# Four steps of weight preparation behind the evictions of a Strassen-Winograd block product, and three operands loaded into their low parts

## The chip, the cores and the metric

The kernel runs on one core of a Trainium2 chip. The metric is the device time of one execution in microseconds; the time before is the median of three runs, 1374.28 us (1374.14 to 1376.15).

## The reference

A two-layer backbone for 1024 latent tokens and 256 context tokens of 1024 channels, in float32: modulated RMS norms, an even layer (a convolution branch and a recurrent branch between one input and one output projection) and an odd layer (pooling). The change touches the even layer's output projection and most of the odd layer's last one:

```python
return jnp.concatenate([y_a, y_b], axis=-1) @ p["w_out"], hT        # even layer
...
z = h @ p["w_in"]                                                   # odd layer
u, g = jnp.split(z, [W_POOL], axis=-1)
...
y = jnp.einsum("bngi,gij->bngj", d, p["w_grp"]).reshape(bn, n, W_POOL) * p["scale"]
return (y * jax.nn.silu(g)) @ p["w_out"]
...
x = x + gate[:, None] * out_x
```

The odd layer's `w_out` is 2048 x 1024. The result must be that of float32 products.

## The kernel before

Activations lie transposed, channels on the 128 partitions and tokens along the row. A float32 product is made of three matmuls on TensorE (PE) in a rounded format, fp32r: each operand v is split into a high part (a cast on ScalarE, ACT, line 95) and a low part v - high (a subtraction on VectorE, DVE, line 96), and high x high, high x low, low x high are summed in PSUM (lines 666, 668, 669).

The large projections are computed in blocks of 256 output channels by 1024 tokens, each by a 2 x 2 Strassen-Winograd scheme: `quad` runs seven products (`prod`, twelve matmuls of 128x512 each) into three PSUM tiles, `qa`, `qb`, `qc` (a, b, c in the code). In the order of the program the products take the weight operands p1, p5, p6, p2, p7, p3, p4 and the token operands b11, t1, t2, b21, t3, b22, t4. Behind most products a PSUM tile is read by `put`, here called an eviction: behind t3's product comes `put(1, 1, b, 1)`, and t4's product, which goes on summing in the same `qb`, must wait for it. Evictions have a high priority. `wquad` prepares the seven weight operands of a block: it loads two raw tiles `wr` of 128x1024, makes sums on DVE (names `ws`, `wr`) and splits seven 128x512 operands (names `wq`). `quad` calls `ahead()`, the preparation of the next block, behind the copy that reads `qa` after the first product (`evac`).

Blocks in order of time: `woa` (layer 1's output projection, first half, m = 0, 2, 4, 6, about 745 to 890 us); then for each of eight m a block `v` and a block `g` of the odd layer's input projection; the weights of these are prepared by `wquad` ahead of the block, not through `ahead`, except that the last `g` block prepares the first block of what follows. The odd layer's output projection has two parts, 1024 input channels each: `wo0` with part 0 (four blocks, m = 0 to 6, from about 1186 us), then `wo1` with part 1 (two blocks in `quad`, the rest in `last_half0` and the code of the end). The evictions are L1088 in `to_gate`, L1150 and L1135 (`gated`) in `wo0`, L1135 in `wo1`.

The token operands of `wo0` and `wo1` come from memory: `y_store` writes the gated blocks and their sums (`y_b`, `y_t`), `y_operand` loads each operand as two raw tiles `yr` of 128x1024 (512 KB) and splits them into `y_<operand>h` and `y_<operand>l`. The raw tiles are taken from a pool shared with other tiles (`xtile`), so a load waits until one is free. All these DMAs are issued by SyncE (SP), in order: an issue that waits holds back all behind it.

A scheduler orders each engine's instructions from the program and from priorities; `tc.issue_after(ins)` keeps what is issued inside it behind `ins` where they are on the same engine. Engines keep that order strictly.

Of the kernel before, what the change touches and what calls it, by code (L numbers as in the profile page):

```python
# [55 lines left out]
def body(ctx, tc, xT, ctxT, cc, ccol, modT, modW, win, gw, wout, wu, grp, wg, wo1, small, edge, ident, outT):  # L56
# [571 lines left out]
    def wquad(src, name, ring, late=False):  # L628
# [17 lines left out]
        nc.vector.tensor_tensor(out=s3, in0=a11, in1=a21, op=sub)  # L646
        nc.vector.tensor_tensor(out=a21, in0=a21, in1=a22, op=add)
# [3 lines left out]
        p6 = op(a11, 6)  # L651
        p2 = op(a12, 2)
        p7 = op(s3, 7)
        nc.vector.tensor_tensor(out=a12, in0=a12, in1=a11, op=sub)
# [5 lines left out]
        return p1, p2, p3, p4, p5, p6, p7  # L660

# [15 lines left out]
    def quad(w, name, ops, put, ahead=None):  # L677
# [14 lines left out]
        w = None  # L692
        if ahead is not None:
            with tc.issue_after(evac.ins):
                w = ahead()
        prod(b, p7, ops["t3"], False, False)
        with tc.high_priority(offset=EVAC):
            put(1, 1, b, 1)
        prod(c, p3, ops["b22"], False, True)
        with tc.high_priority(offset=EVAC):  # L700
            put(0, 1, c, 1)
        prod(b, p4, ops["t4"], False, True)
        with tc.high_priority(offset=EVAC):
            put(1, 0, b, None)
        return w
# [157 lines left out]
    def wo_weights(m):  # L863
        return wquad([wout[m + i, 0] for i in range(2)], f"woa{m}", ring_w)

    w0 = wo_weights(0)
# [16 lines left out]
    def woa(m, w, ahead):  # L883
# [3 lines left out]
        def put(i, h, x, part):  # L887
            v, dr = x1[m + i][:, HALF[h]], x1_part[m + i][:, HALF[h]]
            if part != 1:
                nc.sync.dma_start(v, dr)  # L890
            nc.vector.scalar_tensor_tensor(out=v, in0=x, scalar=m0[:, 0, 2 * KT + m + i : 2 * KT + m + i + 1],
                                           in1=v, op0=mult, op1=add)
            if part != 0:
                nc.sync.dma_start(dr, v)
                square_acc(nacc[h][:, :H], v, (m, i) == (0, h), f"n1q{m}_{i}_{h}")
        return quad(w, f"woa{m}", ya, put, ahead)
# [131 lines left out]

    def y_operand(ops, part, name, raw_tile, alloc):
        hi, lo = [], []  # L1030
        for q in range(2):
            r = raw_tile(f"yr_{part}_{name}_{q}")
            nc.sync.dma_start(r, y_raw[part][name][:, q * S : (q + 1) * S])
            hi.append(alloc(f"y{part}_{name}h{q}", F32R))
            lo.append(alloc(f"y{part}_{name}l{q}", F32R))
            split(r, hi[q], lo[q], nc.vector)
# [5 lines left out]
    def y_operands(part, raws, names=BOPS, alloc=None):  # L1042
        for name in names:
            y_operand(yops[part], part, name, next(raws),
# [12 lines left out]
    def wo1_weights(part, m):  # L1057
        return wquad([wo1[m + i, part] for i in range(2)], f"wo{part}_{m}", wo1_ring,
# [3 lines left out]
    vps, silu = [], [None]  # L1062
    for m in range(0, NK, 2):
# [18 lines left out]
        def to_gate(i, h, x, part):  # L1082
            v = ys[m + i][:, HALF[h]]
            if part == 0:
                keep_part(parts, f"g{m}", i, x)
                return
            if part == 1:
                nc.vector.tensor_tensor(out=v, in0=x, in1=parts[i], op=add)  # L1088
                x = v
            silu[0] = nc.scalar.activation(v, x, AF.Silu)  # L1090

# [16 lines left out]
        if m == NK - 2:  # L1108
            y_operands(0, iter([dtile] + [xtile] * (4 - 1)), BOPS[:4])
# [4 lines left out]
        if m == NK - 2:  # L1114
            with tc.issue_after(silu[0].ins):
                y_operands(0, iter([xtile] * 7), BOPS[4:])
# [21 lines left out]
    for m in range(0, KT, 2):  # L1138
        parts = {}

        def put(i, h, x, part):
# [25 lines left out]
        w = quad(w, f"wo0_{m}", yops[0], put, nxt)  # L1167
        if m == 2:
# [9 lines left out]
    for m in range(0, KT - 4, 2):  # L1178
        def put(i, h, x, part):
            v = x1[m + i][:, HALF[h]]  # L1180
            gated(m + i, v, x)
            if part != 0:
                square_fin(m + i, h, slice(0, H), v)
        def ahead():
# [74 lines left out]
    def last_half0(m, w, ahead=None):  # L1259
# [10 lines left out]
        if ahead is not None:  # L1270
            with tc.issue_after(evac.ins):
                nxt = ahead()
# [159 lines left out]
```

## Time and profile before

| | |
|---|---|
| median of three runs | 1374.28 us (1374.14 to 1376.15) |
| the profiled execution | 1381.07 us, span 1379.3 us, mean granted PE clock 0.974 |
| PE busy | 1295.9 us of the span, 5664 matmuls |
| DVE busy | 1205.1 us, 1587 instructions |
| ACT busy | 632.7 us |
| mean DMA traffic | 132 GB/s |

PE is the engine to watch, but a busy share is a mean over stages: a row of PE whose start is later than the one before it allows, with a wait in brackets behind it, tells where time goes. `<-DVE y L1088` in such a row names the instruction that released it, and why that one was late is read on its own engine. PEclk is the clock that was granted to PE, in tenths or as a share of 1.

### The profile page before, as it was taken

What the parts mean: (1) busy time and instruction counts of PE and PEld (TensorE: products, weight loads), DVE (VectorE), ACT (ScalarE), POOL (GpSimd) and SP (SyncE); (2) the same over time, 40 slices, a digit from 0 to 9 for tenths busy, and PEclk for the clock granted to TensorE, in tenths of its full rate; (3) what the DMA queues carried; (4) which work ended last, traced back from release to release, by engine and by line L of the source; (5) the groups of instructions that cost most, each with busy time, mean ns of one, the idle gap of its engine ahead of it and who ended that gap; (6) DMA issues with size and microseconds to landing.
All of it is one profiled execution on the core that took longest, in us unless ns stands there. A gap on an engine that the chain in (4) does not pass through costs nothing.

```text
span 1379.3 us, 15637 instructions
## 1 busy us (share of the span) xinstructions
PE 1295.9 (94%) x5664; PEld 1048.2 (76%) x5664; DVE 1205.1 (87%) x1587; ACT 632.7 (46%) x906; POOL 363.3 (26%) x182
## 2 busy tenths in 40 slices
PE   7889989898999799999998999999999999999896
PEld 4468868787777587787887887788888888778685
DVE  7998999999999999998778865999999987876775
ACT  6353644674465542304533544754334344634442
POOL 5173534743473555523320004000000000000002
PEclk9899999999999899999999999999999999999997
DMA  9753011111112113343353646424243334758623
GB/s 354 280 180 119 25 59 54 53 40 61 54 35 72 46 46 130 110 151 135 103 185 122 221 154 205 138 93 151 100 145 123 115 115 132 265 190 275 206 107 123
DMA packets 82866, 181.79 MB, mean 132 GB/s; under 512 B 7778, under 2 KB 27618, under 8 KB 82788
## 3 DMA queue, kind: packets, MB, share of 16 engines
q1 hardware_dynamic: 74340, 176.60, 37.8%
q10 hardware_dynamic: 8448, 4.20, 1.0%
q8 instruction: 44, 0.72, 0.2%
q14 instruction: 34, 0.28, 0.1%
HBM read 136.72 MB, written 44.04 MB: 131 GB/s over the span
## 4 chain that ended last, share of the span: by engine, by line
PE 36%; DVE 10%; DMA 7%; issue 2%; ACT 2%; POOL 1%; POOLq 0%; SPq 0%; DVEq 0%; ACTq 0%
PE ga L127 2%; PE ga L128 2%; PE ga L126 2%; PE wob L127 2%; PE wob L128 2%; PE wob L126 2%; DMA wr_g<-wg 1%; DVE ws L986 1%; DMA yr_t<-y_t 1%; DMA wr_v<-wfold 1%; PE qb_g L666 1%; DVE wq_g L96 1%; PE qb_g L669 1%; PE qb_g L668 1%; DVE wq_wo L96 1%
## 5 line engine op out<-in xcount | busy, mean ns | idle before, releaser
L746 DVE SCALAR_TENSOR_TENSOR conv<-u,sm,conv 128x1013 f32<-128x1013 f32 (+14 forms) x232 | 291.2, 1272 | 6.6 <-ACT conv L738 3.8
L1252 POOL TENSOR_TENSOR o<-x,rr 128x256 f32<-128x256 f32 (+1 forms) x9 | 8.0, 923 | 462.9 <-ACT rr L1240 460.0
L511 ACT ACTIVATE g<-g,sm 128x512 f32<-128x512 f32 (+1 forms) x96 | 58.8, 617 | 110.5 <-PE g L510 108.3
L96 POOL TENSOR_TENSOR wl_wu<-wr_wu,wh_wu 128x1024 fp32r<-128x1024 f32 x16 | 39.4, 2470 | 153.9 <-ACT wh_wu L95 147.7
L463 POOL TENSOR_TENSOR g<-g,uc 128x1280 f32<-128x1280 f32 x16 | 47.5, 2967 | 107.9 <-ACT g L511 65.1
L249 PE MATMUL fold<-gh,wh_wu 128*128 128x512 f32 x128 | 53.0, 416 | 5.7 <-ACT wh_wu L95 5.7
L250 PE MATMUL fold<-gl,wh_wu 128*128 128x512 f32 x128 | 52.4, 409 | 3.2 <-DVE gl L96 3.2
L128 PE MATMUL gb<-h0h,wl_gb 128*128 128x512 f32 x128 | 50.7, 398 | 4.8 <-POOL wl_gb L96 4.8
L126 PE MATMUL vg<-h0h,wh_vg 128*128 128x512 f32 x128 | 52.3, 408 | 2.7 <-ACT g L511 2.1
L251 PE MATMUL fold<-gh,wl_wu 128*128 128x512 f32 x128 | 50.7, 405 | 2.3 <-POOL wl_wu L96 2.3
L128 PE MATMUL xb<-h0h,wl_xb 128*128 128x512 f32 x128 | 50.2, 392 | 2.0 <-POOL wl_xb L96 2.0
L127 PE MATMUL wob<-ybl,wh_wob 128*128 128x512 f32 x128 | 50.5, 395 | 1.2 <-POOL ybl L96 1.2
L465 POOL TENSOR_TENSOR g<-g,th 128x1280 f32<-128x1280 f32 x16 | 46.9, 2948 | 16.8 <-ACT th L449 16.8
L127 PE MATMUL vg<-h0l,wh_vg 128*128 128x512 f32 x128 | 51.2, 400 | 0.0
L126 PE MATMUL gb<-h0h,wh_gb 128*128 128x512 f32 x128 | 50.6, 395 | 0.1
L126 PE MATMUL va<-h0h,wh_va 128*128 128x512 f32 x128 | 50.6, 395 | 0.0
L127 PE MATMUL va<-h0l,wh_va 128*128 128x512 f32 x128 | 50.6, 395 | 0.0
L508 PE MATMUL g<-uh,wh_gw 128*128 128x512 f32 (+1 forms) x96 | 36.3, 379 | 15.1 <-ACT wh_gw L95 6.4
L126 PE MATMUL wob<-ybh,wh_wob 128*128 128x512 f32 x128 | 50.6, 396 | 0.0
L128 PE MATMUL wob<-ybh,wl_wob 128*128 128x512 f32 x128 | 49.9, 391 | 0.7 <-POOL wl_wob L96 0.7
L128 PE MATMUL va<-h0h,wl_va 128*128 128x512 f32 x128 | 50.4, 395 | 0.0
L127 PE MATMUL gb<-h0l,wh_gb 128*128 128x512 f32 x128 | 50.4, 393 | 0.0
(548 smaller groups left out, 4301.1 us busy)
## 6 DMA issues: line engine op xcount, KB each, us to landing
mod<-modT SPq DMA_DIRECT2D x28, 512.0 KB, 5.5
wr_wu<-wu SPq DMA_DIRECT2D x16, 512.0 KB, 3.9
x_part<-xp SPq DMA_DIRECT2D x32, 256.0 KB, 2.4
mod<-modT SPq DMA_DIRECT2D x32, 256.0 KB, 3.3
wr_v<-wfold SPq DMA_DIRECT2D x16, 512.0 KB, 3.7
wr_g<-wg SPq DMA_DIRECT2D x16, 512.0 KB, 5.4
wr_wo<-wo SPq DMA_DIRECT2D x16, 512.0 KB, 4.2
yr_t<-y_t SPq DMA_DIRECT2D x16, 512.0 KB, 6.3
```

The lines of the kernel that those rows point to most:

```text
L96: eng.tensor_tensor(out=lo, in0=src, in1=hi.bitcast(F32), op=sub))
L126: nc.tensor.matmul(ps, hi[:, kc], xh[k][:, cols], start=(k == 0), stop=False)
L127: nc.tensor.matmul(ps, hi[:, kc], xl[k][:, cols], start=False, stop=False)
L128: nc.tensor.matmul(ps, lo[:, kc], xh[k][:, cols], start=False, stop=(k == ks - 1))
L249: nc.tensor.matmul(ps, wh[:, kc], gh[i], start=(i == 0), stop=False)
L250: nc.tensor.matmul(ps, wh[:, kc], gl[i], start=False, stop=False)
L251: nc.tensor.matmul(ps, wl[:, kc], gh[i], start=False, stop=(i == 3))
L463: nc.gpsimd.tensor_tensor(out=ius[d], in0=ius[d], in1=uc, op=mult)
L465: nc.gpsimd.tensor_tensor(out=ius[d], in0=ius[d], in1=roots[d], op=mult)
L508: nc.tensor.matmul(ps[:, :n], gwh[:, kc], uh[:, a : a + n], start=True, stop=False)
L511: nc.scalar.activation(t[:, a : a + n], ps[:, :n], AF.Sigmoid, bias=col(ob + d * KT + j))
L746: nc.vector.scalar_tensor_tensor(out=(us[j] if k == 30 else acp)[:, a:b], in0=us[j][:, a + o : b + o], scalar=col(O_CONVW + 31 * j + k), i ...
```

## The change

`wquad` becomes the generator `wquad_steps` with three `yield`s, which cut the preparation into four steps: (1) the loads, p1 and the sum `ws`; (2) two sums, p5 and p6; (3) p2 and p7; (4) one sum, p3 and p4. `quad` runs step 1 behind the copy `evac`, as before, and the later steps behind the evictions of t3's, b22's and t4's products: step 2 behind `put(1, 1, b, 1)`, step 3 behind `put(0, 1, c, 1)`, step 4 behind `put(1, 0, b, None)`. Code that calls `wquad` itself, and `last_half0`, runs all steps in one. In `y_operand` a raw tile can be `None`: the raw operand is then loaded into the tile of its low part and split in place; this is used for t3, b22 and t4 of both parts. Of part 0's operands, t2 and b21 are now issued behind the last gate block (behind its eviction `summed`) and not ahead of it; b21 of part 1 is issued behind the last `wo0` block and not inside its `nxt`; the wait of `nxt` for the last store of y falls away. For this every `put` returns the instruction that reads PSUM, in `woa` too, which the diff leaves out.

```diff
-    def wquad(src, name, ring, late=False):
+    def wquad_steps(src, name, ring, late=False):
         raw = []
...
         nc.vector.tensor_tensor(out=s3, in0=a11, in1=a21, op=sub)
+        yield
         nc.vector.tensor_tensor(out=a21, in0=a21, in1=a22, op=add)
         nc.vector.tensor_tensor(out=a11, in0=a21, in1=a11, op=sub)
         if not late:
             p5 = op(a21, 5)
         p6 = op(a11, 6)
+        yield
         p2 = op(a12, 2)
         p7 = op(s3, 7)
+        yield
         nc.vector.tensor_tensor(out=a12, in0=a12, in1=a11, op=sub)
...
+    class Steps:
+        def __init__(self, work):
+            self.work, self.value = work, None
+        def step(self, after=None):
+            with ExitStack() as octx:
+                if after is not None:
+                    octx.enter_context(tc.issue_after(after.ins))
+                try:
+                    next(self.work)
+                except StopIteration as end:
+                    self.work, self.value = iter(()), end.value or self.value
+        def all(self):
+            while self.value is None:
+                self.step()
+            return self.value
+    def wquad(*args):
+        return Steps(wquad_steps(*args)).all()
...
             put(0, 0, a, None)
-        w = None
-        if ahead is not None:
-            with tc.issue_after(evac.ins):
-                w = ahead()
+        nxt = Steps(ahead()) if ahead is not None else Steps(iter(()))
+        nxt.step(evac)
         prod(b, p7, ops["t3"], False, False)
         with tc.high_priority(offset=EVAC):
-            put(1, 1, b, 1)
+            out = put(1, 1, b, 1)
+        nxt.step(out)
         prod(c, p3, ops["b22"], False, True)
         with tc.high_priority(offset=EVAC):
-            put(0, 1, c, 1)
+            out = put(0, 1, c, 1)
+        nxt.step(out)
         prod(b, p4, ops["t4"], False, True)
         with tc.high_priority(offset=EVAC):
-            put(1, 0, b, None)
-        return w
+            out = put(1, 0, b, None)
+        nxt.step(out)
+        return nxt.all() if ahead is not None else None
...
     def wo_weights(m):
-        return wquad([wout[m + i, 0] for i in range(2)], f"woa{m}", ring_w)
-
-    w0 = wo_weights(0)
+        return wquad_steps([wout[m + i, 0] for i in range(2)], f"woa{m}", ring_w)
+    w0 = Steps(wo_weights(0)).all()
     for name in BOPS[4:]:
...
         for q in range(2):
-            r = raw_tile(f"yr_{part}_{name}_{q}")
-            nc.sync.dma_start(r, y_raw[part][name][:, q * S : (q + 1) * S])
             hi.append(alloc(f"y{part}_{name}h{q}", F32R))
             lo.append(alloc(f"y{part}_{name}l{q}", F32R))
+            r = lo[q].bitcast(F32) if raw_tile is None else raw_tile(f"yr_{part}_{name}_{q}")
+            nc.sync.dma_start(r, y_raw[part][name][:, q * S : (q + 1) * S])
             split(r, hi[q], lo[q], nc.vector)
...
         for name in names:
-            y_operand(yops[part], part, name, next(raws),
+            y_operand(yops[part], part, name, next(raws, None),
                       alloc or (dtile if name in ("b11", "b21", "t4") else d2tile))
...
     def wo1_weights(part, m):
-        return wquad([wo1[m + i, part] for i in range(2)], f"wo{part}_{m}", wo1_ring,
+        return wquad_steps([wo1[m + i, part] for i in range(2)], f"wo{part}_{m}", wo1_ring,
                      part == 1 and m >= KT - 4)
     wo1_ring = wo_ring(iter(["x", "x", "x", "wh", "wl", "wh", "wl"] + ["wh", "wl", "d", "d"] * 14))
-    vps, silu = [], [None]
+    vps, silu, summed = [], [None], [None]
     for m in range(0, NK, 2):
...
                 return
+            out = None
             if part == 1:
-                nc.vector.tensor_tensor(out=v, in0=x, in1=parts[i], op=add)
+                out = summed[0] = nc.vector.tensor_tensor(out=v, in0=x, in1=parts[i], op=add)
                 x = v
             silu[0] = nc.scalar.activation(v, x, AF.Silu)
+            return out
...
         if m == NK - 2:
-            y_operands(0, iter([dtile] + [xtile] * (4 - 1)), BOPS[:4])
+            y_operands(0, iter([dtile, xtile]), BOPS[:2])
         for i in range(2):
             for h in range(2):
                 pool(m + i, h, vps[2 * i + h])
         w = quad(wq, f"g{m}", bx, to_gate, (lambda: wo1_weights(0, 0)) if m == NK - 2 else None)
         if m == NK - 2:
+            with tc.issue_after(summed[0].ins):
+                y_operands(0, iter([xtile] * 2), BOPS[2:4])
             with tc.issue_after(silu[0].ins):
-                y_operands(0, iter([xtile] * 7), BOPS[4:])
+                y_operands(0, iter(()), BOPS[4:])
         for i in range(2):
...
                 x = s
-            gated(m + i, t, x)
+            out = gated(m + i, t, x)
             nc.sync.dma_start(x1_part[m + i][:, HALF[h]], t)
             if (m, i, h) == (0, 0, 1):
                 y_sums(NK - 2)
+            return out
         def nxt():
             if m < KT - 2:
-                with tc.issue_after(stored[0].ins):
-                    return wo1_weights(0, m + 2)
-            w = wo1_weights(1, 0)
-            y_operands(1, iter([xtile]), BOPS[3:4])
-            return w
+                return wo1_weights(0, m + 2)
+            return wo1_weights(1, 0)
         if m == KT - 2:
             with tc.issue_after(loaded[0].ins):
                 y_operands(1, iter([xtile] * 2), BOPS[1:3])
         w = quad(w, f"wo0_{m}", yops[0], put, nxt)
+        if m == KT - 2:
+            y_operands(1, iter([xtile]), BOPS[3:4])
         if m == 2:
...
             v = x1[m + i][:, HALF[h]]
-            gated(m + i, v, x)
+            out = gated(m + i, v, x)
             if part != 0:
                 square_fin(m + i, h, slice(0, H), v)
+            return out
         def ahead():
             if m == 0:
-                y_operands(1, iter([xtile] * 3), BOPS[4:])
-            w = wo1_weights(1, m + 2)
+                y_operands(1, iter(()), BOPS[4:])
+            w = yield from wo1_weights(1, m + 2)
             x2_load(m + 2)
...
             with tc.issue_after(evac.ins):
-                nxt = ahead()
+                nxt = Steps(ahead()).all()
         with tc.issue_after(mm.ins):
```

What the change does to the order, at three places. In the changed file line 1117 is the former L1088, 1152 the former L1120 (the product of gate and pooled tokens), 1167 L1135, 1182 L1150, 1063 L1033 (loads of operands), 1041 L1014 (stores of y), and 648, 649 the former 647, 648.

DVE around the last gate block; `qb_g` and `qc_g` are its PSUM tiles, `y_t2l` and `y_b21l` low parts of part 0's operands, `wq_wo`, `ws_wo` and `wr_wo` the weights of the first `wo0` block. Before:

```order
L96 TENSOR_TENSOR y_t2l_8878<-yr_t_0_8875,y_t2h_8877 128x1024
L647 TENSOR_TENSOR wr_wo_0_1_8974<-wr_wo_0_1_8974 128x512
L96 TENSOR_TENSOR y_t2l_8884<-yr_t_1_8881,y_t2h_8883 128x1024
L96 TENSOR_TENSOR wq_wo_0_1_8976<-wr_wo_0_0_8972,wq_wo_0_1_8976 128x512
L96 TENSOR_TENSOR y_b21l_8890<-yr_b_0_8887,y_b21h_8889 128x1024
L96 TENSOR_TENSOR wq_wo_0_5_8983<-wr_wo_0_1_8974,wq_wo_0_5_8983 128x512
L648 TENSOR_TENSOR wr_wo_0_0_8972<-wr_wo_0_1_8974,wr_wo_0_0_8972 128x512
L96 TENSOR_TENSOR y_b21l_8896<-yr_b_1_8893,y_b21h_8895 128x1024
L1088 TENSOR_TENSOR y_8849<-qc_g_8916,s_g_8957 128x512
L1120 SCALAR_TENSOR_TENSOR y_8849<-vp_6540,sm,y_8849 128x512
L1088 TENSOR_TENSOR y_8850<-qb_g_8917,s_g_8943 128x512
L96 TENSOR_TENSOR wq_wo_0_6_8986<-wr_wo_0_0_8972,wq_wo_0_6_8986 128x512
```

Now:

```order
L96 TENSOR_TENSOR y_t1l_8870<-yr_t_1_8871,y_t1h_8869 128x1024
L646 TENSOR_TENSOR ws_wo_0_8955<-wr_wo_0_0_8948,wr_wo_0_1_8950 128x512
L1152 SCALAR_TENSOR_TENSOR y_8849<-vp_6540,sm,y_8849 128x512
L1117 TENSOR_TENSOR y_8850<-qb_g_8893,s_g_8919 128x512
L648 TENSOR_TENSOR wr_wo_0_1_8950<-wr_wo_0_1_8950 128x512
L1117 TENSOR_TENSOR y_8849<-qc_g_8892,s_g_8933 128x512
L96 TENSOR_TENSOR wq_wo_0_2_8993<-wr_wo_0_0_8948,wq_wo_0_2_8993 128x512
L649 TENSOR_TENSOR wr_wo_0_0_8948<-wr_wo_0_1_8950,wr_wo_0_0_8948 128x512
L1152 SCALAR_TENSOR_TENSOR y_8850<-vp_6549,sm,y_8850 128x512
L96 TENSOR_TENSOR wq_wo_0_5_8973<-wr_wo_0_1_8950,wq_wo_0_5_8973 128x512
```

The two evictions stand ahead of the splits of t2 and b21, which come eight and more rows later, and of the weight splits of steps 2 to 4.

SP at the same time; `y_b_1`, as a target, is a store of y, `yr_t_…_95` and `yr_b_…_96` load t2 and b21, `97`, `98` and `99` are t3, b22 and t4, and `wr_wo_2` is the raw weight of block 2. Before:

```order
L1033 DMA yr_t_0_8875<-y_t_0_95 128x1024
L1033 DMA yr_t_1_8881<-y_t_0_95 128x1024
L1033 DMA yr_b_0_8887<-y_b_0_96 128x1024
L1033 DMA yr_b_1_8893<-y_b_0_96 128x1024
L1033 DMA yr_t_0_9043<-y_t_0_97 128x1024
L1033 DMA yr_t_1_9049<-y_t_0_97 128x1024
L1033 DMA yr_b_0_9055<-y_b_0_98 128x1024
L1033 DMA yr_b_1_9061<-y_b_0_98 128x1024
L1014 DMA y_b_1_100<-y_8849 128x512
L1033 DMA yr_t_0_9067<-y_t_0_99 128x1024
L1014 DMA y_b_1_105<-y_8850 128x512
L1033 DMA yr_t_1_9073<-y_t_0_99 128x1024
```

Now:

```order
L1041 DMA y_b_1_100<-y_8849 128x512
L1063 DMA yr_t_0_9021<-y_t_0_95 128x1024
L1063 DMA yr_t_1_9027<-y_t_0_95 128x1024
L1063 DMA yr_b_0_9033<-y_b_0_96 128x1024
L1063 DMA yr_b_1_9039<-y_b_0_96 128x1024
L1041 DMA y_b_1_105<-y_8850 128x512
L632 DMA wr_wo_2_0_9140<-wo 128x1024
L1041 DMA y_b_1_103<-y_8850 128x512
L1063 DMA y_t3l_9044<-y_t_0_97 128x1024
L632 DMA wr_wo_2_1_9142<-wo 128x1024
L1063 DMA y_t4l_9064<-y_t_0_99 128x1024
L1063 DMA y_t3l_9049<-y_t_0_97 128x1024
```

A store of y stands ahead of t2 and b21, and another two stores and block 2's weights ahead of t3 and t4; b22 comes last, behind the rows shown.

DVE between blocks 2 and 4 of `wo0`; `s_wo_2` is the eviction behind block 2's t3 product, `wq_wo_4` the operands of block 4. Before:

```order
L96 TENSOR_TENSOR wq_wo_4_1_9299<-wr_wo_4_0_9295,wq_wo_4_1_9299 128x512
L96 TENSOR_TENSOR wq_wo_4_2_9312<-wr_wo_4_0_9295,wq_wo_4_2_9312 128x512
L646 TENSOR_TENSOR ws_wo_4_9302<-wr_wo_4_0_9295,wr_wo_4_1_9297 128x512
L1150 TENSOR_TENSOR qc_wo_2_9236<-qc_wo_2_9236,s_wo_2_9277 128x512
L647 TENSOR_TENSOR wr_wo_4_1_9297<-wr_wo_4_1_9297 128x512
L96 TENSOR_TENSOR wq_wo_4_7_9315<-ws_wo_4_9302,wq_wo_4_7_9315 128x512
L648 TENSOR_TENSOR wr_wo_4_0_9295<-wr_wo_4_1_9297,wr_wo_4_0_9295 128x512
L96 TENSOR_TENSOR y_b11l_9378<-yr_b_0_9375,y_b11h_9377 128x1024
L96 TENSOR_TENSOR wq_wo_4_5_9306<-wr_wo_4_1_9297,wq_wo_4_5_9306 128x512
L654 TENSOR_TENSOR wr_wo_4_0_9295<-wr_wo_4_0_9295 128x512
L1150 TENSOR_TENSOR s_wo_2_9263<-qb_wo_2_9237,s_wo_2_9263 128x512
```

Now:

```order
L96 TENSOR_TENSOR wq_wo_4_1_9293<-wr_wo_4_0_9289,wq_wo_4_1_9293 128x512
L1182 TENSOR_TENSOR s_wo_2_9257<-qb_wo_2_9231,s_wo_2_9257 128x512
L1167 SCALAR_TENSOR_TENSOR xp_1_1_9310<-s_wo_2_9257,m_162,xp_1_1_9310 128x512
L646 TENSOR_TENSOR ws_wo_4_9296<-wr_wo_4_0_9289,wr_wo_4_1_9291 128x512
L648 TENSOR_TENSOR wr_wo_4_1_9291<-wr_wo_4_1_9291 128x512
L1182 TENSOR_TENSOR qc_wo_2_9230<-qc_wo_2_9230,s_wo_2_9271 128x512
L649 TENSOR_TENSOR wr_wo_4_0_9289<-wr_wo_4_1_9291,wr_wo_4_0_9289 128x512
L96 TENSOR_TENSOR wq_wo_4_5_9317<-wr_wo_4_1_9291,wq_wo_4_5_9317 128x512
L1167 SCALAR_TENSOR_TENSOR xp_0_1_9335<-qc_wo_2_9230,m_162,xp_0_1_9335 128x512
```

The eviction `s_wo_2` now follows the first split of block 4; before, nine rows of block 4's preparation, a split of b11 and the other eviction stood between.

More of the change, by code (lines that the diff above doesn't have):

```diff
@@ L890, in put @@
                 nc.sync.dma_start(v, dr)
-            nc.vector.scalar_tensor_tensor(out=v, in0=x, scalar=m0[:, 0, 2 * KT + m + i : 2 * KT + m + i + 1],
-                                           in1=v, op0=mult, op1=add)
+            out = nc.vector.scalar_tensor_tensor(out=v, in0=x, scalar=m0[:, 0, 2 * KT + m + i : 2 * KT + m + i + 1],
+                                                 in1=v, op0=mult, op1=add)
             if part != 0:
@@ L1180, in put @@
             v = x1[m + i][:, HALF[h]]
-            gated(m + i, v, x)
+            out = gated(m + i, v, x)
             if part != 0:
                 square_fin(m + i, h, slice(0, H), v)
+            return out
         def ahead():
             if m == 0:
-                y_operands(1, iter([xtile] * 3), BOPS[4:])
-            w = wo1_weights(1, m + 2)
+                y_operands(1, iter(()), BOPS[4:])
+            w = yield from wo1_weights(1, m + 2)
             x2_load(m + 2)
```

## Prediction

> **What bounds the kernel now.** I read the page's busy shares first, then windows over the end of the program, the waits of PE there, and the timelines of PE, DVE and SP around each long wait.
>
> ```profile
> PE 1295.9 (94%) x5664; PEld 1048.2 (76%) x5664; DVE 1205.1 (87%) x1587; ACT 632.7 (46%) x906; POOL 363.3 (26%) x182
> ```
>
> PE bounds. The change leaves its 5664 matmuls alone, so only PE's idle and slowed time can move. In the windows below (length, then busy us of PE, PEld, DVE, ACT, POOL, then PEclk) the stretch before 1160 is full and the later ones are not.
>
> ```profile
> 1120.00:1160.00 40.00, 40.00 (x178) 33.16 (x177) 27.87 (x46) 16.02 (x28) 0.00 (x0) 1.00 0.38 122
> 1160.00:1200.00 40.00, 37.26 (x152) 30.20 (x151) 34.19 (x50) 21.59 (x32) 0.00 (x0) 0.91 0.65 218
> 1200.00:1240.00 40.00, 37.02 (x158) 30.26 (x157) 31.88 (x46) 17.54 (x27) 0.00 (x0) 0.96 0.58 192
> 1280.00:1320.00 40.00, 35.67 (x151) 27.53 (x150) 28.90 (x41) 17.95 (x27) 0.00 (x0) 1.00 0.62 206
> ```
>
> What PE waits for after 1140 (total, times, longest):
>
> ```profile
> PE qb_wo L666 <- DVE s_wo L1150: 3.8, 2, 3.0
> PE qb_g L666 <- DVE y L1088: 2.7, 1, 2.7
> PE qb_wo L666 <- DVE x L1135: 2.1, 2, 1.5
> PE qb_wo L666 <- ACT y_t4h L95: 0.9, 1, 0.9
> PE qb_wo L668 <- DVE y_t4l L96: 0.8, 1, 0.8
> PE qc_wo L668 <- DVE y_b22l L96: 0.8, 1, 0.8
> PE qb_wo L668 <- DVE y_t3l L96: 0.4, 1, 0.4
> ```
>
> The first three are evictions that DVE makes late (8.6 us), the rest operands of part 1 that come late (2.9 us). A wait costs more than itself: in PE's rows (start, duration, wait in brackets) around the first and around L1150's, and at both ends of the stretch with the others, one sees the lost time.
>
> ```profile
> 1186.19 0.39 PE L666 MATMUL qa_wo<-y_b11h,wq_wo 128*128 128x512 f32 x1
> 1188.70 0.39 PE L669 MATMUL qa_wo<-y_b11h,wq_wo 128*128 128x512 f32 x1
> 1191.84 0.80 PE L666 MATMUL qb_g<-x_t4h,wq_g 128*128 128x512 f32 x1 [2.75 <-DVE y L1088]
> 1196.70 0.63 PE L669 MATMUL qb_g<-x_t4h,wq_g 128*128 128x512 f32 x1
> 1198.25 0.39 PE L666 MATMUL qc_wo<-y_t1h,wq_wo 128*128 128x512 f32 x1
> ...
> 1232.72 0.39 PE L669 MATMUL qa_wo<-y_b11h,wq_wo 128*128 128x512 f32 x1
> 1236.09 0.79 PE L666 MATMUL qb_wo<-y_t4h,wq_wo 128*128 128x512 f32 x1 [2.98 <-DVE s_wo L1150]
> 1240.30 0.40 PE L666 MATMUL qc_wo<-y_t1h,wq_wo 128*128 128x512 f32 x1
> ...
> 1285.00 0.39 PE L666 MATMUL qc_wo<-y_t1h,wq_wo 128*128 128x512 f32 x1
> 1303.65 0.39 PE L666 MATMUL qc_wo<-y_t1h,wq_wo 128*128 128x512 f32 x1
> ```
>
> Undisturbed matmuls start 0.228 us apart (1186.19 to 1188.70 is eleven steps); a product of twelve is 2.7 us. Stall A (1191.84): sixteen steps from 1188.70 should end at 1192.34 and end at 1198.25, so A costs 5.9 us, of which 2.75 is the wait and the rest matmuls at 0.44 (1191.84 to 1196.70 is eleven steps). Stall B (1236.09): thirteen steps from 1232.72 should end at 1235.7 and end at 1240.30, so 4.6. Stall D: 55 matmuls lie between 1285.00 and 1303.65 and should take 12.5 of those 18.65 us, so 6.1, of which 4.4 is waits: short waits cost 1.4 times themselves. Two small ones are left: C, the other L1150 wait (0.9, about 1.2 in all), and E, the other L1135 wait (0.6, about 0.9).
>
> [...]
>
> **The change part by part.** The same loads, sums, casts and splits are issued, none added, except that three raw tiles fall away; every edit is a move.
>
> *Steps, last gate block and first block of part 0 (A).* DVE's rows around A:
>
> ```profile
> 1184.62 1.23 DVE L96 TENSOR_TENSOR y_t2l<-yr_t,y_t2h 128x1024 fp32r<-128x1024 f32 x1 [0.68 <-ACT y_t2h L95]
> 1186.36 1.22 DVE L96 TENSOR_TENSOR y_b21l<-yr_b,y_b21h 128x1024 fp32r<-128x1024 f32 x1
> 1188.70 1.22 DVE L96 TENSOR_TENSOR y_b21l<-yr_b,y_b21h 128x1024 fp32r<-128x1024 f32 x1
> 1191.10 0.68 DVE L1088 TENSOR_TENSOR y<-qb_g,s_g 128x512 f32<-128x512 f32 x1
> ```
>
> The t3 product of the gate is through at about 1186.4, but its eviction stands behind the splits of t2 and b21 and runs at 1191.10. In the new order it stands ahead of them: about 1186.6, t4 follows b11 at 1188.93 without a wait, and the 5.9 is gone. But the operand loads go later on SP's queue. Now:
>
> ```profile
> 1172.93 6.03 SPq L1033 DMA_DIRECT2D yr_t<-y_t  x3
> 1179.06 2.89 SPq L1033 DMA_DIRECT2D yr_b<-y_b  x2
> 1183.66 4.27 SPq L1033 DMA_DIRECT2D yr_t<-y_t  x2
> 1188.02 2.25 SPq L1033 DMA_DIRECT2D yr_b<-y_b  x2
> 1197.36 0.32 SPq L1033 DMA_DIRECT2D yr_t<-y_t  x1
> ...
> yr_t<-y_t SPq DMA_DIRECT2D x16, 512.0 KB, 6.3
> yr_b<-y_b SPq DMA_DIRECT2D x11, 512.0 KB, 5.0
> ```
>
> Afterwards the t2 loads stand behind a store of y that waits for DVE (1183.4, estimate), b21 at 1186.2, t3 behind the next block's weight load and a store that waits for the last y (1194.4 and 1197.7), t4 1197.3 and 1202, b22 1202.4 and 1204.2, some 14 us later than now. Walking DVE in the new order with 0.60 us for a 128x512 operation and 1.14 for a 128x1024 split (the spacing of the DVE rows): thirteen short ones after 1186.6, so t2's first low part at 1195.0, where PE wants it at 1194.35: 0.7 us. The t3 low parts end near 1201.7 and 1205 (landing 5, cast 1.05, split 1.22); twelve b11 matmuls of the next block cover 2.7 of it: 1.5 us. The eviction behind the splits of t4 and t3: 0.95. The second half of b22: 1.2. Sum 4.35, by 1.4 is 6.1. A nets 0. Bounds: landing at the high 6.3 in four serial places is 5 worse; all in time would be 5.9 better, and since every load is later I take half of that: -5 to +4.
>
> *Steps, blocks of part 0 (B, C).* DVE's rows around B:
>
> ```profile
> 1228.80 1.29 DVE L96 TENSOR_TENSOR wq_wo<-wr_wo,wq_wo 128x512 fp32r<-128x512 f32 x2 [2.58 <-ACT wq_wo L95]
> 1233.01 1.22 DVE L96 TENSOR_TENSOR y_b11l<-yr_b,y_b11h 128x1024 fp32r<-128x1024 f32 x1
> 1235.35 0.68 DVE L1150 TENSOR_TENSOR s_wo<-qb_wo,s_wo 128x512 f32<-128x512 f32 x1
> ```
>
> The eviction of the t3 product (through at 1230.4: twelve matmuls before 1232.72) waits behind everything prepared for block 4. Afterwards only block 4's first split (loaded at about the present time, so at 1228.8, or up to 1 us later for the longer SP queue) is ahead of it: 1230.7 to 1231.3 instead of 1235.35, with b11's product covering until 1232.95. PE still needs 0.24 us and 0.68 after it: at most 0.5 us of wait, 0.7 with its slow part. B gains 3.9; bounds 2.4 (the wait halves only, with its slow part) and 4.6. C: block 6's b11 product now comes before t3 and no longer covers the eviction: 0.24 + 0.68 = 0.95 us open, and two t1 products that come right behind cost 0.3 and 0.45 more. 1.7 by 1.4 is 2.4, against 1.2 now: -1.2, bounds -2.5 and +0.5.
>
> *Part 1's first block (D, E).*
>
> ```profile
> 1287.39 1.23 DVE L96 TENSOR_TENSOR y_t3l<-yr_t,y_t3h 128x1024 fp32r<-128x1024 f32 x1 [2.06 <-ACT y_t3h L95]
> 1288.53 0.75 DVE L1135 SCALAR_TENSOR_TENSOR x<-qb_wo,m,x 128x512 f32<-128x512 f32 x1
> ```
>
> DVE waited 2.06 us for an operand with PE's eviction behind it. The three operands now load into their own low tiles, which come free when PE has read part 0's (b22 and t3 of block 6, about 1270 and 1275) and not when a raw tile is free; so t3's load leaves some 5 us earlier than now, b22's 6 to 8, t4's stays late behind a weight load. The new order puts b22 ahead of t3 on PE, which takes 3 us back. I count 1.6 us of waits, 2.2 in all, against 6.1: D gains 4.0. Bounds: 0, if the loads only change places, and 6.1. E gains 0.8 since b11 of the next block stands behind t3 now; bounds 0 and 0.9.
>
> *Layer 1's output projection (745 to 890).* The same steps. PE waits little there:
>
> ```profile
> PE qc_woa L666 <- ACT wq_woa L95: 2.5, 1, 2.5
> PE qc_woa L669 <- DVE wq_woa L96: 1.0, 1, 1.0
> ```
>
> Both are the first block's, whose weights are still prepared in one piece. Two evictions stand behind one split more (0.68 at most), and the loads of the fold that follows leave about 1 us later: -0.7, bounds -2.5 and +0.5. Between 890 and 1160 no order changes that PE waits for: 0, with 1 us either way. The last half blocks run all steps at once as now: 0.
>
> Sum: 0 + 3.9 - 1.2 + 4.0 + 0.8 - 0.7 = 6.8 us. The profiled execution took 1381.07 (its span 1379.3), 0.5% over the median 1374.28; the stalls are of the order of waits, so I subtract the same 6.8 from the median: 1367.5.
>
> **The rivals.** (1) *The stalls all go.* Part 0's operands land in time after all, because PE is itself 6 us nearer to its evictions and the DMA share is 0.58 to 0.65: A is +5 in place of 0, giving about 1362. For it: PE holds 2.7 us per product in reserve. Against it: b22's last load leaves 7 us after the present last one (1197.36).
>
> (2) *Slower: part 0's first block waits for its operands.* SP issues in order, and t3, t4 and b22 stand behind two stores that wait for DVE and two weight loads. Every landing that is late puts PE in a wait, and each wait over 2.7 us brings eleven matmuls at 0.44 with it, 2.3 us more. Three such waits of 3.5 us are 17.4; the sum then is 6.8 + 6.1 - 17.4 = -4.5, 1378.8. It decides from 6.1 + 6.8 + 2.75 = 15.7 us of lost time in that block on. For it: the present kernel puts those loads first, and t4's (1197.36) is used within some 15 us. Against it: twelve matmuls of the next block stand ready to fill.
>
> [...]
>
> (3) *The wait moves to the weights.* Step 2 comes behind the t3 eviction, so p5 for the next t1 product is six DVE operations and a cast later: 6 x 0.60 + 0.62 = 4.2 us. Where the order leaves only t4 (2.7) in between, t1 waits 1.5 with its slow part 2.1, at up to nine block changes: 19 us, 1386. With b11 in between too (5.4) it costs nothing, and that is how most blocks stand; four uncovered block changes take back the gain: about 1376, unchanged.
>
> **How the numbers follow.** A measurement of this kernel can tell about 0.2%, 2.75 us. Forecast (gain 3 to 10) 0.47, rival 1 (10 or more) 0.18, no change 0.13 (half of it rival 3), slower 0.22 (rival 2 0.15, rival 3 0.07). Faster 0.65, same 0.13, slower 0.22. The forecast's own range is 1363 to 1371. For 8 in 10 it needs rival 1's end (1362 less 1) and most of the slower cases: 1361 to 1378.
>
> **What would show it.** A: no wait for the gate's eviction near 1188, but waits of qb_wo and qc_wo for y_t2l, y_t3l and y_b22l in the first block, sum about 4.4. B: no wait for L1150's counterpart above 1 us in blocks 2 and 4, one of about 1 in the blocks around. D: the counterparts of y_t3l, y_b22l, y_t4l under 1.6 us together. PE busy in windows of 40 us from 1160 on: above 38. The prediction is wrong if a qb_wo or qc_wo wait for an operand's low part is above 3 us, if t1 products wait for wq, or if the woa blocks wait for their evictions by more than 1.5 us in all.

## The result, and the profile after

The changed kernel is slower: 1386.76 us median (1383.29 to 1389.06) against 1374.21 us for the kernel before, ratio 1.0086, interval 1.0062 to 1.011. That is 12 us, under one per cent, where 6.8 us less was forecast, and it lies above the end of the predicted range (1378). The profiled execution took 1385.91 us, its span 1384.1.

What PE waits for after 1140 (total, times, longest), to be set against the list of before. In the changed file L691, L693, L694 are the matmuls, L1182 and L1167 the former L1150 and L1135:

```profile
PE qc_wo L691 <- DVE xp L1167: 5.2, 1, 5.2
PE fin_ms L1260 <- DVE fin L1252: 3.4, 2, 2.0
PE qc_wo L691 <- ACT qb_wo L707: 2.2, 1, 2.2
PE qb_wo L691 <- DVE s_wo L1182: 1.6, 2, 0.8
PE qa_wo L691 <- ACT wq_wo L95: 0.6, 1, 0.6
PE qb_wo L691 <- ACT y_t3h L95: 0.5, 1, 0.5
PE qb_wo L693 <- DVE y_t2l L96: 0.5, 1, 0.5
PE qc_wo L691 <- ACT y_t4h L95: 0.4, 1, 0.4
PE qc_wo L693 <- DVE y_b22l L96: 0.4, 2, 0.2
```

The 2.7 us for the gate's eviction and the 3.0 us for L1150 are gone, and part 1's operands cost little. In their place stand 5.2 and 2.2 us ahead of t1 products. The windows of 40 us show the same (length, busy us of PE, PEld, DVE, ACT, POOL, then PEclk):

```profile
1160.00:1200.00 40.00, 39.52 (x174) 32.40 (x174) 31.60 (x49) 20.98 (x32) 0.00 (x0) 1.00 0.54 178
1200.00:1240.00 40.00, 36.52 (x148) 26.47 (x146) 28.23 (x38) 16.31 (x25) 0.00 (x0) 1.00 0.69 232
1240.00:1280.00 40.00, 33.71 (x138) 27.12 (x139) 25.48 (x35) 14.84 (x24) 0.00 (x0) 0.91 0.68 231
1280.00:1320.00 40.00, 37.73 (x160) 29.44 (x159) 32.41 (x45) 20.52 (x31) 0.00 (x0) 1.00 0.62 225
```

PE gained 2.3 us in the first and 2.1 in the last, and lost 5.4 in the third, which read before:

```profile
1240.00:1280.00 40.00, 39.14 (x173) 32.09 (x172) 28.27 (x40) 17.36 (x26) 0.00 (x0) 1.00 0.76 258
```

How the 5.2 us came about is read from DVE and SP of the changed kernel. First PE, then DVE, then SP, and last what SP's load of the old sum waited for; the rows are picked out:

```profile
1260.52 0.39 PE L691 MATMUL qa_wo<-y_b21h,wq_wo 128*128 128x512 f32 x1
1266.35 0.77 PE L691 MATMUL qc_wo<-y_t1h,wq_wo 128*128 128x512 f32 x1 [5.21 <-DVE xp L1167]
```

```profile
1251.09 0.69 DVE L96 TENSOR_TENSOR wq_wo<-wr_wo,wq_wo 128x512 fp32r<-128x512 f32 x1 [3.62 <-ACT wq_wo L95]
1255.04 0.69 DVE L646 TENSOR_TENSOR ws_wo<-wr_wo,wr_wo 128x512 f32<-128x512 f32 x1 [3.25 <-DMA wr_wo<-wo]
1255.65 0.75 DVE L1167 SCALAR_TENSOR_TENSOR xp<-qa_wo,m,xp 128x512 f32<-128x512 f32 x1
1265.45 0.75 DVE L1167 SCALAR_TENSOR_TENSOR xp<-qc_wo,m,xp 128x512 f32<-128x512 f32 x1 [6.46 <-DMA xp<-x_part]
```

```profile
1245.76 0.33 SPq L632 DMA_DIRECT2D wr_wo<-wo  x1
1248.33 0.42 SPq L632 DMA_DIRECT2D wr_wo<-wo  x1
1248.80 2.86 SPq L1063 DMA_DIRECT2D yr_t<-y_t  x4
1256.42 0.32 SPq L1185 DMA_DIRECT2D x_part<-xp  x1
1262.27 0.32 SPq L1178 DMA_DIRECT2D xp<-x_part  x1
```

```profile
SPq L1178 <- DMA x_part<-xp: 5.4, 1, 5.4
```

Block 6's raw weights left at 1245.76 and 1248.33. DVE waited 3.62 and 3.25 us for them, and the eviction of `qa` (1255.65) stood behind. The store of its sum left at 1256.42, behind six loads of 512 KB. The next old sum, `xp`, is loaded into one of only two buffers; this one had to wait until that store had landed, and left 5.85 us after it. DVE waited 6.46 us for it, `qc` was held, and PE waited for `qc`. The 2.2 us near 1241 end in the same way: the row names a copy on ACT, but the t1 product there also needs `qc`, released by L1167 at 1240.93. There DVE waited only 0.49 us for the old sum; the longer wait ahead of it, 2.59 us at 1232.81, was for block 4's weights.

The same 6.46 us held the rest of block 6's preparation. In `wo0` what `put` returns is not the read of PSUM but the update behind it (`gated`, L1167), which needs the old sum, so the later steps stand behind the arrival of old sums as well. The raw weights of part 1's first block left at 1271.43 and 1273.07; before, at 1255.59.

A second trace of the kernel before (experiment 5) sets the scale: the two executions differ by 4.4 us, almost all of it ahead of 745 us, where PE is busy 691.76 us in one and 695.28 in the other; nothing of the change lies there. So traces are compared by stages here, not by their spans.

### The profile page after: what moved, and what is told of

It reads as the page before. It is cut to its first block, busy times and chain, and to the rows that moved or that the text cites. A ratio compares the mean times of both kernels' runs of the same rounds, so it can differ in the third digit from the quotient of the medians.

```text
span 1384.1 us, 15605 instructions
## 1 busy us (share of the span) xinstructions
PE 1295.0 (94%) x5664; PEld 1044.2 (75%) x5664; DVE 1204.9 (87%) x1587; ACT 632.1 (46%) x906; POOL 362.3 (26%) x182
## 4 chain that ended last, share of the span: by engine, by line
PE 37%; DVE 10%; DMA 8%; issue 1%; ACT 1%; POOL 0%; SPq 0%; POOLq 0%; DVEq 0%; ACTq 0%
DMA x_part<-xp 2%; PE ga L128 2%; PE ga L126 2%; PE ga L127 2%; PE wob L128 2%; PE wob L127 2%; PE wob L126 2%; DMA xp<-x_part 1%; DVE ws L1013 1%; PE qb_g L691 1%; PE qb_g L693 1%; PE qb_g L694 1%; PE qb_v L691 1%; PE fold L250 1%; PE fold L251 1%
## 5 line engine op out<-in xcount | busy, mean ns | idle before, releaser
L95 ACT CAST wq_g<-wr_g 128x512 fp32r<-128x512 f32 x48 | 28.2, 620 | 50.6 <-DMA wr_g<-wg 17.0
```

The lines of the kernel that those rows point to most:

```text
L95: return (nc.scalar.copy(hi, src), eng.tensor_tensor(out=lo, in0=src, in1=hi.bitcast(F32), op=sub))
```

## The experiments

All ratios are to the kernel before, with 95% intervals; the changed kernel stands at 1.0086. A difference between two kernels is the difference of their ratios, put into us. Each kernel but the one before has one trace.

**1 and 2. Steps alone, operand moves alone.** Kernel 1 undoes the operand edits (part 1's b21 and the dropped wait for the last store of y stay as changed):

```diff
-            y_operands(0, iter([dtile, xtile]), BOPS[:2])
+            y_operands(0, iter([dtile] + [xtile] * (4 - 1)), BOPS[:4])
...
-            with tc.issue_after(summed[0].ins):
-                y_operands(0, iter([xtile] * 2), BOPS[2:4])
             with tc.issue_after(silu[0].ins):
-                y_operands(0, iter(()), BOPS[4:])
+                y_operands(0, iter([xtile] * 7), BOPS[4:])
...
-                y_operands(1, iter(()), BOPS[4:])
+                y_operands(1, iter([xtile] * 3), BOPS[4:])
```

> The four steps alone: the operands t2, b21 ahead of the last gate block and t3, b22, t4 through raw tiles, as in the kernel before. Theory S (the steps cost, through the next block's weights that arrive later and push SP's loads of the old sums, xp, behind the operand loads): slower than before by 6 us or more, a wait of qc_wo for the eviction that reads xp above 2 us. Theory L (the low-part loads and the late issue of part 0's operands cost): within 4 us of the kernel before or faster.

Kernel 2 keeps them and runs the steps at once, behind the copy `evac`:

```diff
-        nxt.step(evac)
+        if ahead is not None:
+            with tc.issue_after(evac.ins):
+                nxt.all()
...
-        nxt.step(out)
```

> The operand loads of the changed kernel, but the next block's weights prepared in one piece behind the copy of qa. Theory S: within 4 us of the kernel before, and no wait above 2 us for an xp eviction. Theory L: slower by 6 us or more, with waits of qb_wo and qc_wo for y_t3l, y_t4l or y_b22l in part 0's first block.

Measured: 1392.54 us, 1.0122 (1.0095 to 1.0148), and 1371.18 us, 0.9966 (0.9953 to 0.998). The steps cost some 16.8 us, the operand moves gain 4.7, and the two add up to the 12 us of the change. Theory L falls. The evictions still hold PE in kernel 1 (L1180, L1165 and L1117 are the former L1150, L1135 and L1088), and the old sums do so too, as theory S expected:

```profile
PE qb_wo L691 <- DVE s_wo L1180: 4.4, 2, 2.3
PE qc_wo L691 <- DVE xp L1165: 2.2, 1, 2.2
PE qb_g L691 <- DVE y L1117: 1.7, 1, 1.7
```

The waits of PE after 1170 in kernel 2, beside those of the tail (3.4 and 0.5 us; L735 copies sums out of PSUM):

```profile
PE qa_wo L691 <- ACT wq_wo L95: 2.4, 1, 2.4
PE qa_wo L691 <- ACT s_wo L735: 1.9, 1, 1.9
PE qb_wo L691 <- ACT s_wo L735: 1.7, 1, 1.7
```

No eviction by DVE is on it, neither the gate's nor L1150's, although the weights are prepared in one piece. So the stalls that the prediction gave to the steps go without the steps, and the steps alone do not take them away.

**3. Layer 1's output projection in one piece**, all else as changed (`whole` runs all four steps at once):

```diff
-        w0 = woa(m, w0, (lambda: wo_weights(m + 2)) if m < KT - 2 else None)
+        w0 = woa(m, w0, (lambda: whole(wo_weights(m + 2))) if m < KT - 2 else None)
```

> The changed kernel, but the blocks of layer 1's output projection prepare their next weights in one piece. The trace after lost about 4 us against the one before between 750 and 881 us. If the steps there cost that, this is 3 to 5 us faster than the changed kernel; if they only move waits that the fold takes back, the same within 1 us.

Measured: 1379.51 us, 1.0029 (1.0012 to 1.0046): 0.57%, 7.8 us under the changed kernel, more than expected. The window 745 to 890, first of before, then of the changed kernel, then of this one:

```profile
745.00:890.00 145.00, 140.93 (x614) 114.37 (x612) 112.36 (x176) 76.14 (x125) 19.89 (x10) 0.99 0.51 166
```

```profile
745.00:890.00 145.00, 137.29 (x595) 110.59 (x594) 111.51 (x165) 76.18 (x126) 20.05 (x12) 0.99 0.50 160
```

```profile
745.00:890.00 145.00, 140.46 (x611) 113.83 (x610) 115.25 (x175) 78.38 (x129) 20.34 (x14) 0.99 0.52 171
```

PE loses 3.6 us there with the steps and gets 3.2 back without. What it waited for in the changed kernel, beside the first block's weights, which are the same in both:

```profile
PE ms_n L193 <- DVE n1acc L907: 1.3, 1, 1.3
PE qc_v L693 <- DVE x_t1l L96: 1.2, 2, 0.9
PE fold L249 <- ACT wh_wu L95: 1.1, 1, 1.1
PE qb_woa L691 <- DVE x L917: 0.6, 2, 0.4
```

Evictions (L917) are the smallest of them. The fold that follows loads its raw weights into the same pair of tiles; no run shows that this is what delays it. The 3.6 us are one trace: with the four steps in these blocks PE is busy 138.17, 139.01 and 139.04 us in that window in kernels 1, 4 and 9, and 140.41 to 141.22 in the seven traces without. More is lost behind the window: from 890 to 1183 PE is busy 0.83 us less than in the trace of before. The table behind the experiments has both together.

**4. Four buffers for the old sums**, two of them the accumulators that stand idle then:

```diff
-            t = vtile(f"xp{m}_{i}_{h}")
+            xps.append(0)
+            t = (vtile if len(xps) % 2 else atile)(f"xp{m}_{i}_{h}")[:, :H]
```

> The changed kernel, with the old sums xp of the wo0 blocks in four buffers and not two, two of them the idle accumulators; nothing else is changed. Theory S' (the waits of 2.2 us near 1239 and 5.2 us near 1261 are xp loads that wait for the store of the sum in the same buffer): both waits go, 8 to 11 us less than the changed kernel. If the loads are late because SP stands or the DMA is full, whatever the buffer, the waits stay and it is the same within 2 us.

Measured: 1383.97 us, 1.0072 (1.0055 to 1.009), some 2 us less and not 8 to 11; the intervals overlap. The waits of PE for `xp` are gone from the list, as expected, but L1184 (the former L1150) is back with 3.0. DVE shows what took their place. Its waits from 1200 to 1280, in the changed kernel and then here:

```profile
DVE xp L1167 <- DMA xp<-x_part: 10.7, 5, 6.5
DVE wq_wo L96 <- ACT wq_wo L95: 6.2, 2, 3.6
DVE ws_wo L646 <- DMA wr_wo<-wo: 3.7, 2, 3.3
```

```profile
DVE wq_wo L96 <- ACT wq_wo L95: 10.5, 4, 4.1
DVE ws_wo L646 <- DMA wr_wo<-wo: 6.7, 3, 3.0
```

10.7 us for old sums are gone and the 9.9 for weights have become 17.2. The ring of two was the last of two delays, not the only one.

**5. The kernel before again**, unchanged.

> The kernel before, unchanged, for a second trace. The profiled execution of before was 6.9 us above its median. If its lost time lies in the output projection (stalls whose length varies with the transfers), the windows 1183 to 1330 lose less than 18.8 us here; if it lies before 700 us, they lose the same and the stretch before 700 loses less than 55.2 us.

Measured: 1376.66 us, once. The stalls are there again (2.7 for L1088, 2.7 for L1150), and from 745 on both traces lose the same within 1 us; the difference lies ahead of 745.

**6. Steps 2 to 4 together** behind the t3 eviction:

```diff
-        nxt.step(out)
+        if ahead is not None:
+            with tc.issue_after(out.ins):
+                nxt.all()
...
-        nxt.step(out)
...
-        nxt.step(out)
```

> The changed kernel with steps 2, 3 and 4 run together behind the eviction of the t3 product; only step 1 is apart. Theory W (the later steps hold the two raw weight tiles until the t4 product, so that the next loads leave some 6 us later, and DVE, waiting for them in step 1, holds the evictions behind it): the raw tiles come free about 5 us earlier, and the time falls by 4 us or more against the changed kernel. If the wait for the old sums or for part 0's operands is what costs, it stays within 2 us of it.

Measured: 1382.7 us, 1.0057 (1.0035 to 1.008), 4 us under the changed kernel, with intervals that overlap: it does not settle the question.

**7. t2 and b21 early, low parts kept, weights in one piece** (with the edit of kernel 2):

```diff
-            y_operands(0, iter([dtile, xtile]), BOPS[:2])
+            y_operands(0, iter([dtile] + [xtile] * (4 - 1)), BOPS[:4])
...
-            with tc.issue_after(summed[0].ins):
-                y_operands(0, iter([xtile] * 2), BOPS[2:4])
```

> Weights in one piece, t3, b22 and t4 loaded to their low parts, but t2 and b21 of part 0 issued ahead of the last gate block as before. If the gain of the kernel with all operand moves (0.34%) comes from the later t2 and b21, which leave DVE free for the gate's eviction, that stall of 2.7 us is back here and the time is 4 us or more above it; if it comes from part 1's low-part loads, the time is the same within 2 us.

Measured: 1374.3 us, 0.998 (0.9964 to 0.9997). The gate's stall is back, 2.7 us as before, but the time is only 1.9 us above kernel 2, not 4 or more. The two kernels differ elsewhere too: here PE also waits 4.0 us for old sums:

```profile
PE qa_wo L691 <- DVE xp L1164: 4.0, 2, 2.9
PE qb_g L691 <- DVE y L1116: 2.7, 1, 2.7
```

So the later t2 and b21 are enough to take the gate's stall away; the steps alone (kernel 1) leave 1.7 us of it.

**8. Weights in one piece, operand moves, four buffers** (edits 2 and 4 together).

> Weights in one piece, all operand moves, and the old sums in four buffers. If the ring of two holds the loads of the old sums back in this kernel too, it is 2 to 4 us faster than without the buffers; its waits left (2.4 for weights, 1.9 and 1.7 for copies of sums) do not name the old sums, which speaks for no change within 1 us.

Measured: 1367.94 us, 0.9932 (0.9911 to 0.9953), 4.7 us under kernel 2 (the intervals touch), although none of kernel 2's PE waits named the old sums. DVE waited 10.2 us for them there from 1200 to 1280, and has no such wait here.

**9 and 11. Raw weights of blocks 2 and 6 in tiles of their own**, with four buffers; 9 with the steps, 11 with weights in one piece:

```diff
-            r = wpool.tile([P, D], F32, tag="wr", name=f"wr_{name}_{i}")
+            r = (raws or wr_tile)(f"wr_{name}_{i}")
...
-                     part == 1 and m >= KT - 4)
+                     part == 1 and m >= KT - 4, xtile if part == 0 and m in RAWX else None)
+    RAWX = (2, 6)
```

> The changed kernel with the old sums in four buffers and the raw weights of wo0's blocks 2 and 6 in two tiles of their own (blocks 4 and 0 of part 1 keep the old pair), so that the loads of a block leave before the steps of the block before are through. Theory W (raw tiles held by the later steps): the weight waits and the eviction wait of 3.0 us at the change to part 1 go, 6 us or more below the kernel with four buffers alone. If the steps cost by where their DVE operations stand, it stays within 2 us of that kernel.

> Weights in one piece, all operand moves, four buffers for the old sums and separate raw tiles for blocks 2 and 6. In one piece the raw tiles are free soon after the copy of qa, so theory W gives little: within 2 us of the same kernel without them (ratio 0.9932). If loads of weights were late whatever the steps, the waits for weights of 1.5 and 0.4 us go and it is 2 to 4 us faster.

Measured: 9 takes 1382.44 us, 1.0042 (1.0024 to 1.0061), 4 us under kernel 4, between the two forecasts and at the edge of the intervals. On DVE its waits for weights from 1200 to 1280 fell from 17.2 us to 3.1, but on SP the second half of t3 now stands behind the store of the first sum and left at 1202.79, not at 1199.08 as in kernel 4, and PE waited for t3 (L694 and L696 are matmuls):

```profile
PE qb_wo L696 <- DVE y_t3l L96: 2.8, 1, 2.8
PE qb_wo L694 <- ACT y_t3h L95: 2.7, 1, 2.7
```

11 takes 1362.48 us, 0.9896 (0.9856 to 0.9936), the lowest of all, 14 us under the kernel before. It is 5 us under kernel 8, where theory W had expected at most 2, but these two intervals overlap; if the gain is real, the raw tiles hold loads back in one piece too. PE's windows there:

```profile
1160.00:1200.00 40.00, 40.00 (x177) 32.66 (x176) 37.01 (x53) 24.77 (x37) 0.00 (x0) 1.00 0.77 272
1200.00:1240.00 40.00, 39.35 (x174) 32.26 (x173) 31.88 (x48) 16.18 (x26) 0.00 (x0) 1.00 0.72 241
1240.00:1280.00 40.00, 38.85 (x169) 31.04 (x167) 33.38 (x44) 22.85 (x31) 0.00 (x0) 1.00 0.78 283
1280.00:1320.00 40.00, 40.00 (x177) 33.12 (x177) 31.07 (x49) 18.81 (x31) 0.00 (x0) 1.00 0.30 105
```

**10. Only step 4 late**, steps 1 to 3 in one piece:

```diff
         nxt.step(evac)
+        nxt.step(evac)
+        nxt.step(evac)
...
-            out = put(1, 1, b, 1)
-        nxt.step(out)
+            put(1, 1, b, 1)
...
-            out = put(0, 1, c, 1)
-        nxt.step(out)
+            put(0, 1, c, 1)
```

> The changed kernel with steps 1 to 3 in one piece behind the copy of qa, and only step 4 (one sum, p3 and p4, the last reads of both raw tiles) behind the t4 eviction. Theory W: the raw tiles come free as late as in the changed kernel, so it costs 8 us or more against weights in one piece with the same operand loads (ratio 0.9966), ratio 1.002 or above. If steps 2 and 3 behind their evictions are what costs, it is near that kernel, ratio 0.995 to 0.999.

Measured: 1383.62 us, 1.0051 (1.0029 to 1.0073). Against kernel 2 (0.9966) it costs 0.85%, 11.7 us: the late last step alone, which holds the last reads of both raw tiles, brings most of what the four steps cost. It makes the operands p3 and p4 late too, and this run does not separate the two. What holds PE, besides the tail, are mostly weights and copies that come late:

```profile
PE qc_wo L691 <- ACT wq_wo L95: 2.3, 1, 2.3
PE qb_wo L691 <- ACT s_wo L736: 2.3, 1, 2.3
PE qa_wo L691 <- ACT wq_wo L95: 1.9, 1, 1.9
PE qb_wo L691 <- DVE s_wo L1182: 1.5, 2, 0.9
```

This is what theory W asked for in time. The loads bear it out in part only. Counted from the start of the first product of the block before, the raw weights of part 1's first block leave after 11.9 us here, 8.2 in kernel 2 and 19.4 in the changed kernel, and block 4's after 14.1, 12.9 and 22.3; but block 6's after 12.0, 13.9 and 12.9, no later than in one piece.

**The stages of all traces**, in us: from PE's first `woa` product to its first `wo0` product, and from there to the matmul of the final norm.

| kernel | steps in `woa` | `woa` to `wo0` | `wo0` to norm |
|---|---|---|---|
| before, twice | none | 435.2, 435.8 | 167.9, 168.2 |
| changed | four | 440.7 | 169.6 |
| 1 | four | 442.1 | 176.8 |
| 4 | four | 438.9 | 166.2 |
| 9 | four | 441.5 | 167.8 |
| 6 | two | 439.6 | 169.8 |
| 10 | last late | 441.1 | 168.1 |
| 3 | none | 435.3 | 169.4 |
| 2 | none | 435.5 | 159.5 |
| 7 | none | 434.2 | 162.7 |
| 8 | none | 435.7 | 157.4 |
| 11 | none | 433.2 | 152.6 |

Late steps in `woa` cost 3 to 9 us ahead of `wo0`, 5.7 on average, whatever else is changed; kernel 3, which has them everywhere else, loses nothing there. From `wo0` on the operand moves gain 8.6 us (kernel 2) and the steps take 10.2 back; the last step alone takes 8.7. By one trace each, tiles of their own for raw weights gain 4.8 us in one piece (11 against 8) and nothing with the steps (9 against 4), so with the steps the raw tiles are not shown to be the limit. The changed kernel loses 6 to 7 us in these stages, of the 12 between the medians. The other 5 the traces do not place; the two executions of before differ by 4.4 us, almost all of it ahead of 745 us.

## Why the prediction was wrong

**Failed: the evictions after block 2 (B).** The step "only block 4's first split (loaded at about the present time, or up to 1 us later)" did not hold. The loads left at 1227.06 and 1230.42, and not at 1221.58. The eviction itself held nothing up, but the stretch lost 3.7 us instead of the forecast 0.7 (4.6 before): a wait of 0.6 us for the weights, the 2.2 us for `qc`, and the slow matmuls behind both (three starts 0.33 to 0.39 us apart behind the first, one of 0.31 behind the second, 0.228 undisturbed). I had counted what the steps take off DVE's queue ahead of an eviction, and not that they keep the raw tiles, and with them the next loads, until the last step. The second load was held longer still: the last split of the old weights ended at 1227.66, and the load left right behind that of an old sum (1230.05).

**Failed: C, whose sum left out a term.** Forecast 2.4 us; the change from block 4 to block 6 lost 7.7, and that to part 1 another 1.6. The 5.2 us wait for the old sum is no row of the prediction. The DVE waits of before for `xp`, from 1200 to 1280, were there to read, and so was the ring of two; I took them for idle time of an engine with reserve:

```profile
DVE xp L1135 <- DMA xp<-x_part: 5.7, 4, 2.0
```

They became 10.7. Four buffers (experiment 4) take PE's wait away but give back only some 2 us of the time, so the ring is not the whole of it.

**Failed: layer 1's output projection.** Forecast -0.7 with an end of -2.5. PE loses 3.6 us in the window, the way from `woa` to `wo0` is some 5 us longer, and 7.8 us of time come back when the steps there are taken out. I priced two evictions and about 1 us for the fold's loads, and put what comes between 890 and 1160 at 0. The fold and the norm wait; why is open, and that the fold's loads share the raw tiles is only a likely reason.

**Right in size, with another cause: A.** The gate's eviction came in time and the first block lost 4.9 us by PE's rows against the 6.1 forecast (net +1, forecast 0). But experiments 2 and 7 show that the late t2 and b21 are enough to remove the stall, and experiment 1 that the steps alone leave 1.7 us of it. The size is partly luck: the waits there add up to 2.2 us and not to 4.35, and the starts around them (0.56 to 1.17 us to the matmul that waited, then 0.34 to 0.52 to the next, 0.228 undisturbed) helped to make the loss 2.3 times the waits, not 1.4.

**Right in size: D and E.** D lost 2.4 us (forecast 2.2, before 6.1) and E nothing. Experiment 2 confirms that operand moves alone gain, by 4.7 us. But t3's loads hardly left earlier: at 1277.89 and 1283.58, against 1278.51 and 1280.21 before. Part of the help is that PE came to this block 3 us later.

**The rivals.** Rival 2 (operands late in the first block) did not happen: no wait there above 0.8 us. Rival 3 came near in time (its full price was 1386), but not by its own way: the one wait of a t1 product for a weight is 0.2 us, and in the traces most of the loss lies ahead of `wo0`. So the match is chance. The three signs of being wrong hardly showed either (low parts at most 0.5 us, t1 products and weights 0.2, evictions in `woa` 0.6): they watched the delays that the sum had counted.

**What stays open.** That the steps cost, that the last one brings most of it, and that old sums and raw weights take each other's place as the last delay is shown. How the 16.8 us divide between the held raw tiles, the late operands p3 and p4 and the other order of DVE and SP that the steps bring is not: own raw tiles with the steps gave 4 us at the edge of the intervals, none of it in the traces from `wo0` on, and a new wait for t3. For layer 1's projection nothing of the kind was run.

In these traces the length of a wait does not fix how slow the matmuls behind it are. Undisturbed they start 0.228 us apart. In the profiled execution of before, thirteen starts 0.43 us apart followed the wait of 2.75 us (1192.43 to 1197.98, PEclk 0.91 from 1160 to 1200), but only five the wait of 2.98 us (1236.68 to 1238.82, PEclk 0.96 from 1200 to 1240). In the changed kernel eight followed the 5.21 us wait (1266.91 to 1270.32, PEclk 0.91 in that window). A wait of 2.94 us in kernel 7 (1266.65) was followed by starts at most 0.31 us apart, and one of 1.57 us in kernel 6 (1200.13) by nine that were 0.43 us or more apart. The eleven slow matmuls that rival 2 adds to each wait over 2.7 us were my estimate from the wait of 2.75 us alone, and are no rule.

## What to carry to other kernels

Work that is cut into steps holds its input buffers until the last step: here block 4's raw weights left at 1227.06 and 1230.42, before at 1221.58. Before it is spread out, look for who loads next into the same buffers, and when; a stall taken off one engine can come back as a late load: the 2.7 and 3.0 us for evictions went here, and 5.2 us for an old sum came. Waits of an engine that has reserve are worth reading when evictions stand behind them: a ring of two for small load-and-store tiles cost 4.7 us here with the weights in one piece (0.9966 against 0.9932). Price the parts of a change separately: the moves of operands were worth 4.7 us, and two buffer changes beside them another 9.6 (0.9896 against 0.9966).

## What was not expected of the hardware

The stretch ahead of 745 us differs by 3.5 us of PE time between two executions of the same program (691.76 and 695.28 busy). A store of 256 KB that left behind six loads of 512 KB was 5.85 us on the way until the load behind it could leave, where such transfers took 2.1 us as a median in the same trace.
